# Twelve gate and up operands stored whole in the first half and split in place in the unit that reads them first

## The chip, the cores and the metric

One core of a Trainium2 chip runs the kernel. The metric is the device time of one execution in microseconds (us), the median of several. A core has five engines that work side by side, each through its own list of instructions in order: PE (matrix multiplications; the loading of its weights is shown apart, as PEld), DVE (vector), ACT (scalar functions, copies), POOL (a second vector engine) and SP, which here issues all DMA transfers. Engines wait for each other, and for transfers, at semaphores.

## The reference

A decoder block on a 2048 x 1024 input in float32: two token mixers in parallel, an output projection and a residual, and then the part that matters here, the gated feed-forward layer:

```python
h2 = rmsnorm(x, norm2_g[l])
ffn = (jax.nn.silu(h2 @ w_ffn_gate[l]) * (h2 @ w_ffn_up[l])) @ w_ffn_down[l]
x = x + ffn
return rmsnorm(x, norm_f_g)
```

`h2` is 2048 x 1024, `w_ffn_gate` and `w_ffn_up` are 1024 x 2816, `w_ffn_down` is 2816 x 1024.

## The kernel before

Every float32 operand of a matrix product is split in two numbers of a shorter format (fp32r): a high part, which ACT makes with a copy (line 153), and a low part, the difference, which DVE makes (line 154). One product is then three matmuls of 128 x 128 weights by 128 x 512 values (lines 391 to 393): high by high, high by low, low by high.

The large products are done in *units* (`unit`, L396): a product of two by two blocks from seven block products instead of eight. `PRODUCTS` names the seven pairs in their order: weights A11, S1, S2, A12, S3, S4, A22 with values B11, T1, T2, B21, T3, B22, T4. Each value operand is four tiles (k = 0 to 3) of 128 x 512, each held as a pair, 128 x 2 x 512, of high and low part, in the pool `opp` of 28 tiles: 7 x 4, so one set fills it. `unit_weights` loads a unit's raw weights by one transfer of 1 MB into one of two `raw` tiles, forms the sums on POOL (lines 374, 375, 376, 381) and splits seven weights into tiles `wq` (a pool of four). Copies of a block (line 413), sums of blocks (line 417) and, for the gate, a silu on ACT (line 452) end a unit.

The positions are done in two halves of 1024. `ffn_up(half)` runs 11 steps of two units each, gate and up; their product is split into `so` tiles (a pool of three, `fo`) by `store_split` and stored (`sa...`). `ffn_down(half)` follows. The second half's `h2` operands are made while `ffn_up(0)` runs: the generator `h2_ahead` is resumed once in four block products and calls `combine`, which for each k loads four blocks of x (`h`), scales them on DVE (line 520) and forms T1 to T4 on POOL (lines 269, 273, 276, 282). Each of the 28 results goes through `put`, which calls `store_split`: an ACT split and a DVE split into a `so` tile, and a store of 512 KB into the DRAM tile `sh<name>_<k>`. A round for one k has seven results: B11, T1, T2, T3, B21, T4, B22.

Between `ffn_down(0)` and `ffn_up(1)`, `load_h2` brings the 28 pairs back into `opp` tiles (28 loads of 512 KB). They are issued on SP among the stores of the first half's last results (`sx`) and the loads of raw weights, behind the raw load of the first gate unit.

The program text gives what is done; the order of each engine's list comes from a scheduler that sorts the instructions by an estimate of their times. It is fixed when the program is built. It lets the products of two neighbouring units overlap: at the place of the change PE's list has products of the up unit (marked ' below: A11', S1' and so on) between those of the gate unit.

In `in_proj` the first layer's operands T3, B22 and T4 (`WHOLE`) already travel whole: `h1_ahead` stores 256 KB, and `load_whole` (L566) loads them into the low part's place and splits them there.

Of the kernel before, what the change touches and what calls it, by code (L numbers as in the profile page):

```python
# [10 lines left out]
F32 = mybir.dt.float32  # L11
# [7 lines left out]
P = 128  # L19
D = 1024  # L20
SEQ = 2048
PB = 512
# [21 lines left out]
WHOLE = ("T3", "B22", "T4")  # L44
# [7 lines left out]
def tile_hymba_block(ctx, tc, x, xt, win, wa, wgu, wout, wffn, wdown, wdown_first, small, out):  # L52
# [3 lines left out]
    def pool_of(name, bufs, **kw):  # L56
        return ctx.enter_context(tc.tile_pool(name=name, bufs=bufs, **kw))
# [8 lines left out]
    dram = pool_of("dram", 1, space=DRAM)  # L66
# [34 lines left out]
    def scratch(name, n):  # L101
# [16 lines left out]
        for half in range(2)  # L118
    ]
    s_h2 = {n: [dram.tile([P, PB], F32, name=f"sf{n}_{k}") for k in range(4)] for n in LATER}  # L120
    s_h2p = {
        n: [dram.tile([P, 2, PB], F32, name=f"sh{n}_{k}") for k in range(4)] for _, n in PRODUCTS
    }

    def made_ahead(name, n):
        return dram.tile([P, PB] if n in WHOLE else [P, 2, PB], F32, name=name)

    s_h1 = {
        n: [made_ahead(f"si{n}_{k}", n) for k in range(4)] for _, n in PRODUCTS
    }  # L130
# [4 lines left out]
    def bank(name="mm"):  # L135
        return ps.tile([P, PB], F32, name=name, tag="mm")

    def tt(name):
        return tp.tile([P, PB], F32, name=name, tag="t")
# [4 lines left out]
    def load(dst, src):  # L144
        return nc.sync.dma_start(dst, src)

    def store(dst, src):
        return nc.sync.dma_start(dst, src)
# [3 lines left out]
    def split(src, hi, lo):  # L152
        last_hi[:] = [act.activation(hi, src, AF.Copy)]  # L153
        return dve.tensor_tensor(lo, src, hi.bitcast(F32), ALU.subtract)  # L154
# [20 lines left out]
    def both_rstd(ssq, rb):  # L175

        tot = [bank("tot") for _ in range(2)]
        for j in range(2):
            pe.matmul(tot[j][:], ones[:], ssq[j][:], start=True, stop=True)
        l, y0 = [[bt(n) for _ in range(2)] for n in ("l", "y0")]  # L180
        with tc.issue_after(last_silu[0].ins):
            last_exp[:] = [act.preload_act_table_set("natural_log_exp_and_others")]
        for j in range(2):
            with tc.issue_after(last_exp[0].ins):
                last_exp[:] = [
                    act.activation(l[j][:], tot[j][:], AF.Ln, bias=eps[:], scale=1.0 / D)
                ]
# [53 lines left out]
    def no_operands():  # L241
        return {b: [] for _, b in PRODUCTS}
# [125 lines left out]
    def unit_weights(src, raw=None):  # L368
        raw = raw_weights(src) if raw is None else raw
        n = src.shape[-1]  # L370
        a11, a12, a22, a21 = [raw[:, i, :] for i in range(4)]
        s1 = rawp.tile([P, PB], F32, name="s1", tag="s1", bufs=1)[:, 0:n]
        w = {"A11": weight_quarter(a11)}
        pool.tensor_tensor(s1, a21, a22, ALU.add)  # L374
        pool.tensor_tensor(a21, a11, a21, ALU.subtract)  # L375
        pool.tensor_tensor(a11, s1, a11, ALU.subtract)  # L376
        w["S1"] = weight_quarter(s1)
        w["S2"] = weight_quarter(a11)
        w["A12"] = weight_quarter(a12)
        w["S3"] = weight_quarter(a21)  # L380
        pool.tensor_tensor(a12, a12, a11, ALU.subtract)  # L381
        w["S4"] = weight_quarter(a12)
        w["A22"] = weight_quarter(a22)
        return w

    def product_step(o, w, op, k, first, s=slice(0, PB)):
        n = len(op)
        c = slice(k * P, (k + 1) * P)
        wh, wl = w[:, 0, c], w[:, 1, c]
        xh, xl = op[k][:, 0, s], op[k][:, 1, s]  # L390
        pe.matmul(o[:, s], wh, xh, start=first and k == 0, stop=False, skip_group_check=True)  # L391
        pe.matmul(o[:, s], wh, xl, start=False, stop=False, skip_group_check=True)  # L392
        return pe.matmul(o[:, s], wl, xh, start=False, stop=k == n - 1, skip_group_check=True)  # L393

    def unit(src, ops, into=None, raw=None, onto=None):


        w = unit_weights(src, raw)

        def mul(i, o=None):  # L400
            first = o is None
            o = bank() if first else o
            n, m = PRODUCTS[i]
            for k in range(len(ops[m])):
                product_step(o, w[n], ops[m], k, first)
            tick()
            return o

        def copied(name, o, at):
            if onto is not None:  # L410
                return plus(onto[at], o)
            t = tt(name) if into is None else into[at]
            act.activation(t[:], o[:], AF.Copy)  # L413
            return t

        def plus(t, o):
            dve.tensor_tensor(t[:], o[:], t[:], ALU.add)  # L417
            return t


        oa = mul(0)
        c11 = copied("c11", oa, (0, 0))
        ob = mul(1)
        c22 = copied("c22", ob, (1, 1))
        mul(2, oa)
        c12 = copied("c12", oa, (0, 1))
        plus(c11, mul(3))
        mul(4, oa)
        plus(c22, oa)
        mul(5, ob)  # L430
        plus(c12, ob)
        mul(6, oa)
        if into or onto:
            copied("c21", oa, (1, 0))
        return [(0, 0, c11, False), (1, 1, c22, False), (0, 1, c12, False), (1, 0, oa, True)]
# [6 lines left out]
        act.activation(s[:], c[:], AF.Copy)  # L442
        return s

    last_silu, last_exp = [], []

    def silu(c, in_psum):
        s = tt("sg") if in_psum else c
        with ExitStack() as stack:
            if last_exp:  # L450
                stack.enter_context(tc.issue_after(last_exp[0].ins))
            last_silu[:] = [act.activation(s[:], c[:], AF.Silu)]
        return s
# [440 lines left out]
    def h2_ahead(ssq):  # L894


        for _ in range(3):
            yield
        rb = [bank("rb_ps") for _ in range(2)]
        yield from both_rstd(ssq, rb)  # L900

        def put(n, k, h):
            store_split(s_h2p[n][k], h)

        yield from combine(lambda k, j: s_x1[2 + j][k][:], C_G2, rb, put)

    def load_h2():
        ops, loads = no_operands(), raw_loads[-1]
        for _, n in PRODUCTS:
            for k in range(4):  # L910
                o = opp.tile([P, 2, PB], F32R, name="op", tag="op")
                with tc.issue_after(loads.ins):
                    load(o[:].bitcast(F32), s_h2p[n][k][:])
                ops[n].append(o)
        return ops

    def ffn_up(half, ops, raw=None):
        for m in range(NF // 2):
            us = unit(wffn[2 * m], ops, raw=None if m else raw)
            sg = {(r, j): silu(c, p) for r, j, c, p in us}  # L920
            for r, j, c, _ in unit(wffn[2 * m + 1], ops):
                s = sg[r, j]
                dve.tensor_tensor(s[:], c[:], s[:], ALU.mult)
            b11, b12, b21, b22 = [sg[r, j] for r in range(2) for j in range(2)]
            t1, t2, t3, t4 = [bt(n) for n in ("t1", "t2", "t3", "t4")]
            for y, p, q in ((t1, b12, b11), (t2, b22, t1), (t3, b22, b12), (t4, b21, t2)):
                pool.tensor_tensor(y[:], p[:], q[:], ALU.subtract)  # L927
            values = [("B11", b11), ("B21", b21), ("B22", b22)]
            if half == 1 and m >= LAST_GROUP:
                values.append(("B12", b12))  # L930
            values += [("T1", t1), ("T2", t2), ("T3", t3), ("T4", t4)]
            background.insert(0, split_later(s_act[half][m], values))
# [235 lines left out]
    ops, first, differences = build_h()  # L1168
# [9 lines left out]
    ops = load_pairs(s_h1)  # L1178
# [124 lines left out]
```

## Time and profile before

| | us |
|---|---|
| median of 3 runs | 2085.23 |
| lowest and highest of them | 2084.04, 2087.19 |
| the profiled execution, its own time | 2085.32 |
| its span, first to last instruction | 2083.6 |
| PE busy in it | 2026.7 |
| DVE busy | 1429.0 |
| ACT busy | 965.2 |
| POOL busy | 882.6 |

Times in views of the trace count from the start of the span. In a row of a timeline stand the start, the duration, the engine, the line of the program, the operation, the tile written and those read, and in brackets the idle time of the engine just before and what ended it. `ffn_up(0)` with the making of the operands ahead lies at about 820 to 1130 us; the seam between the halves, where the operands are loaded, at about 1400 to 1456 us. Matmuls overlap: a row's duration is longer than the step from one start to the next.

### The profile page before, as it was taken

What the parts mean: (1) busy time and instruction counts of PE and PEld (TensorE: products, weight loads), DVE (VectorE), ACT (ScalarE), POOL (GpSimd) and SP (SyncE); (2) the same over time, 40 slices, a digit from 0 to 9 for tenths busy, and PEclk for the clock granted to TensorE, in tenths of its full rate; (3) what the DMA queues carried; (4) which work ended last, traced back from release to release, by engine and by line L of the source; (5) the groups of instructions that cost most, each with busy time, mean ns of one, the idle gap of its engine ahead of it and who ended that gap; (6) DMA issues with size and microseconds to landing.
All of it is one profiled execution on the core that took longest, in us unless ns stands there. A gap on an engine that the chain in (4) does not pass through costs nothing.

```text
span 2083.6 us, 26960 instructions
## 1 busy us (share of the span) xinstructions
PE 2026.7 (97%) x9175; PEld 1651.2 (79%) x9175; DVE 1429.0 (69%) x2057; ACT 965.2 (46%) x1918; POOL 882.6 (42%) x642
## 2 busy tenths in 40 slices
PE   5999999999999999999999999999999999999997
PEld 4778888887888887778888878887888888878886
DVE  7669786549754696787887566654776776666665
ACT  6455455656543245554555442223455444443234
POOL 3427322222102364555555434533655534534545
PEclk9999999999999999999999999999999999999999
DMA  7349495424586882654654587689454465398763
GB/s 277 126 152 313 145 342 160 152 96 137 182 304 206 331 295 96 234 218 175 237 222 163 211 344 275 237 328 361 167 185 159 177 227 202 136 354 318 288 263 121
DMA packets 190395, 464.45 MB, mean 223 GB/s; under 512 B 19952, under 2 KB 67248, under 8 KB 180656
## 3 DMA queue, kind: packets, MB, share of 16 engines
q1 hardware_dynamic: 190256, 462.72, 61.5%
q8 instruction: 72, 1.18, 0.2%
q14 instruction: 67, 0.55, 0.1%
HBM read 297.49 MB, written 165.15 MB: 222 GB/s over the span
## 4 chain that ended last, share of the span: by engine, by line
PE 79%; DVE 6%; DMA 3%; issue 2%; POOL 1%; ACT 1%; SPq 0%; DVEq 0%; POOLq 0%; ACTq 0%
PE mm L391 23%; PE mm L393 23%; PE mm L392 22%; PE mm L824 3%; PE mm L825 2%; PE mm L827 2%; DVE wq L154 2%; DVE so L154 1%; DMA raw<-in_wffn_dram 1%; DMA shT<-so 1%; PE o_ps L748 1%; PE o_ps L750 1%; DMA op<-sa_T 1%; PE sc L724 0%; POOL t L927 0%
## 5 line engine op out<-in xcount | busy, mean ns | idle before, releaser
L391 PE MATMUL mm<-op,wq 128*128 128x512 f32 x2511 | 982.1, 393 | 10.8 <-ACT c L413 5.0
L392 PE MATMUL mm<-op,wq 128*128 128x512 f32 x2511 | 977.3, 389 | 0.0
L393 PE MATMUL mm<-op,wq 128*128 128x512 f32 x2511 | 964.8, 390 | 10.4 <-DVE wq L154 10.2
L154 DVE TENSOR_TENSOR wq<-raw,wq 128x512 fp32r<-128x512 f32 (+2 forms) x626 | 503.0, 810 | 230.7 <-ACT wq L153 228.6
L153 ACT ACTIVATE wq<-raw 128x512 fp32r<-128x512 f32 (+2 forms) x626 | 363.8, 587 | 590.2 <-PE mm L393 456.2
L391 PEld LDWEIGHTS mm<-op,wq 128*128 128x128 f32 x2511 | 472.4, 188 | 122.7 <-ACT c L413 8.6
L393 PEld LDWEIGHTS mm<-op,wq 128*128 128x128 f32 x2511 | 472.5, 188 | 116.7 <-DVE wq L154 18.8
L392 PEld LDWEIGHTS mm<-op,wq 128*128 128x128 f32 x2511 | 472.7, 188 | 96.4 <-issue 1.2
L376 POOL TENSOR_TENSOR raw<-s,raw 128x512 f32<-128x512 f32 (+2 forms) x97 | 127.1, 1310 | 473.4 <-DVE wq L154 446.9
L417 DVE TENSOR_TENSOR y<-mm,y 128x512 f32<-128x512 f32 x185 | 127.2, 689 | 131.5 <-PE mm L393 131.2
L374 POOL TENSOR_TENSOR s<-raw 128x512 f32<-128x512 f32 (+2 forms) x97 | 128.0, 1320 | 205.3 <-DMA raw<-in_wffn_dram 101.4
L381 POOL TENSOR_TENSOR raw<-raw 128x512 f32<-128x512 f32 (+2 forms) x97 | 124.9, 1288 | 164.7 <-DVE wq L154 157.6
L417 DVE TENSOR_TENSOR c<-mm,c 128x512 f32<-128x512 f32 x198 | 135.3, 683 | 64.9 <-PE mm L393 63.6
L806 POOL TENSOR_TENSOR ssx<-ssx,q 128x512 f32<-128x512 f32 x52 | 76.1, 1478 | 161.6 <-ACT q L805 161.5
L375 POOL TENSOR_TENSOR raw<-raw 128x512 f32<-128x512 f32 (+2 forms) x97 | 135.8, 1400 | 5.3
L413 ACT ACTIVATE c<-mm 128x512 f32<-128x512 f32 x198 | 114.9, 587 | 17.3 <-PE mm L393 15.8
L154 DVE TENSOR_TENSOR so<-t,so 128x512 fp32r<-128x512 f32 x100 | 89.1, 896 | 25.2 <-ACT so L153 24.7
L153 ACT ACTIVATE wq<-s 128x512 fp32r<-128x512 f32 (+2 forms) x97 | 56.7, 585 | 95.9 <-PE mm L393 89.0
L824 PE MATMUL mm<-op,wq 128*128 128x512 f32 x256 | 100.9, 395 | 0.0
L825 PE MATMUL mm<-op,wq 128*128 128x512 f32 x256 | 99.8, 390 | 0.0
L154 DVE TENSOR_TENSOR wq<-s,wq 128x512 fp32r<-128x512 f32 (+2 forms) x97 | 81.1, 836 | 9.8 <-ACT wq L153 9.2
L153 ACT ACTIVATE so<-t 128x512 fp32r<-128x512 f32 x100 | 62.5, 627 | 41.6 <-DMA sa_B<-so 17.8
(188 smaller groups left out, 1847.9 us busy)
## 6 DMA issues: line engine op xcount, KB each, us to landing
raw<-in_wffn_dram SPq DMA_DIRECT2D x44, 1024.0 KB, 5.6
sa_T<-so SPq DMA_DIRECT2D x88, 512.0 KB, 5.3
op<-sa_T SPq DMA_DIRECT2D x88, 512.0 KB, 9.6
sa_B<-so SPq DMA_DIRECT2D x69, 512.0 KB, 3.4
op<-sa_B SPq DMA_DIRECT2D x69, 512.0 KB, 9.6
raw<-in_win_dram SPq DMA_DIRECT2D x23, 1024.0 KB, 5.5
raw<-in_wdown_dram SPq DMA_DIRECT2D x24, 768.0 KB, 6.2
sx<-y SPq DMA_DIRECT2D x48, 256.0 KB, 3.0
```

Of the source, the lines that this page charges most:

```text
L153: last_hi[:] = [act.activation(hi, src, AF.Copy)]
L154: return dve.tensor_tensor(lo, src, hi.bitcast(F32), ALU.subtract)
L374: pool.tensor_tensor(s1, a21, a22, ALU.add)
L375: pool.tensor_tensor(a21, a11, a21, ALU.subtract)
L376: pool.tensor_tensor(a11, s1, a11, ALU.subtract)
L381: pool.tensor_tensor(a12, a12, a11, ALU.subtract)
L391: pe.matmul(o[:, s], wh, xh, start=first and k == 0, stop=False, skip_group_check=True)
L392: pe.matmul(o[:, s], wh, xl, start=False, stop=False, skip_group_check=True)
L393: return pe.matmul(o[:, s], wl, xh, start=False, stop=k == n - 1, skip_group_check=True)
L417: dve.tensor_tensor(t[:], o[:], t[:], ALU.add)
L824: pe.matmul(o[e, j][:], wh, m[:, 0, :], start=k == 0, stop=False)
L825: pe.matmul(o[e, j][:], wh, m[:, 1, :], start=False, stop=False)
```

## The change

For T3, B22 and T4 (twelve of the 28 tiles) `put` no longer splits. The tile is stored as it is, 256 KB, into a DRAM tile of half the size. `load_h2` loads it into the low part's half of its `opp` tile. The split is made in the first unit that reads it, the gate unit of step 0 in the second half: a new dictionary `late` holds the four tiles of each name under the index of its product (4, 5, 6), and `mul(i)` calls `split_whole` on them just before the product. ACT writes the high part, and DVE overwrites the value with the low part.

```diff
+    s_h2p = {
+        n: [made_ahead(f"sh{n}_{k}", n) for k in range(4)] for _, n in PRODUCTS
+    }
...
             n, m = PRODUCTS[i]
+            split_whole(late.pop(i, ()))
             for k in range(len(ops[m])):
                 product_step(o, w[n], ops[m], k, first)
...
-    last_silu, last_exp = [], []
+    last_silu, last_exp, late = [], [], {}
...
         def put(n, k, h):
-            store_split(s_h2p[n][k], h)
+            if n in WHOLE:
+                store(s_h2p[n][k][:], h[:])
+            else:
+                store_split(s_h2p[n][k], h)
...
                 with tc.issue_after(loads.ins):
-                    load(o[:].bitcast(F32), s_h2p[n][k][:])
+                    load((o[:, 1, :] if n in WHOLE else o[:]).bitcast(F32), s_h2p[n][k][:])
                 ops[n].append(o)
         return ops
 
+    def split_whole(ops):
+        for o in ops:
+            split(o[:, 1, :].bitcast(F32), o[:, 0, :], o[:, 1, :])
+
     def ffn_up(half, ops, raw=None):
         for m in range(NF // 2):
+            if half and m == 0:
+                late.update({i + 2: ops[n] for i, n in enumerate(WHOLE)})
             us = unit(wffn[2 * m], ops, raw=None if m else raw)
```

The number of instructions on each engine is unchanged: twelve ACT and twelve DVE splits move from `ffn_up(0)` to the start of `ffn_up(1)`. The scheduler also sets some neighbours in another order. Three places are shown, first the list before, then the list now.

The first place is ACT's list in the first half, in the round of k = 0, from the split of an FFN step's T2 (`so<-t_7996`) to the silu at the end of its next gate unit. `so<-t_7897` is the operand T4 and `so<-h` the operand B22; `so<-t_7997` and `so<-t_7998` are the FFN step's own T3 and T4.

```order
L153 ACTIVATE so<-t_7996 128x512
L153 ACTIVATE wq<-s_8158 128x512
L153 ACTIVATE so<-t_7897 128x512
L452 ACTIVATE c_8082<-c_8082 128x512
L153 ACTIVATE wq<-raw 128x512
L452 ACTIVATE c_8063<-c_8063 128x512
L153 ACTIVATE so<-t_7997 128x512
L153 ACTIVATE wq<-raw 128x512
L153 ACTIVATE so<-t_7998 128x512
L153 ACTIVATE so<-h 128x512
L452 ACTIVATE sg<-mm 128x512
```

Now (the lines below the edit have moved by one, L452 to L453):

```order
L153 ACTIVATE so<-t_7996 128x512
L153 ACTIVATE wq<-s_8155 128x512
L153 ACTIVATE so<-t_7997 128x512
L453 ACTIVATE c_8079<-c_8079 128x512
L153 ACTIVATE wq<-raw 128x512
L453 ACTIVATE c_8063<-c_8063 128x512
L153 ACTIVATE so<-t_7998 128x512
L153 ACTIVATE wq<-raw 128x512
L453 ACTIVATE sg<-mm 128x512
```

The two operand splits are gone, and the FFN step's T3 and T4 have each moved up by one place.

The second place is ACT's list at the seam, from the gate unit's first silu (`c_12666`, now `c_12630`, the block c11) on. The `wq` rows behind it are the up unit's weights A11', S1', S2' and so on.

```order
L452 ACTIVATE c_12666<-c_12666 128x512
L153 ACTIVATE wq<-raw 128x512
L153 ACTIVATE wq<-s_12759 128x512
L153 ACTIVATE wq<-raw 128x512
L452 ACTIVATE c_12681<-c_12681 128x512
L153 ACTIVATE wq<-raw 128x512 x3
L452 ACTIVATE c_12695<-c_12695 128x512
L452 ACTIVATE sg<-mm 128x512
```

Now:

```order
L453 ACTIVATE c_12630<-c_12630 128x512
L153 ACTIVATE wq<-raw 128x512
L153 ACTIVATE op<-op 128x512 x5
L153 ACTIVATE wq<-s_12747 128x512
L153 ACTIVATE op<-op 128x512 x2
L153 ACTIVATE wq<-raw 128x512
L153 ACTIVATE op<-op 128x512 x2
L453 ACTIVATE c_12645<-c_12645 128x512
L153 ACTIVATE op<-op 128x512 x2
L153 ACTIVATE wq<-raw 128x512 x2
L453 ACTIVATE c_12667<-c_12667 128x512
L153 ACTIVATE op<-op 128x512
```

The twelve splits (`op<-op`: four of T3, four of B22, four of T4) stand between the up unit's weights, five of them ahead of S1'. DVE's list has its twelve in the same way: five ahead of S1', two ahead of the sum of c22, four after S2' and the last after S3'.

The third place is PE's list at the same time. `wq_12760` (now `wq_12748`) is A11' and `wq_12639` (now `wq_12603`) is S3; `op_12599` (now `op_12563`) is T3 of k = 0.

```order
L391 MATMUL mm_12785<-op_12567,wq_12760 128x512
L392 MATMUL mm_12785<-op_12567,wq_12760 128x512
L393 MATMUL mm_12785<-op_12567,wq_12760 128x512
L391 MATMUL mm_12785<-op_12569,wq_12760 128x512
L391 MATMUL mm_12649<-op_12599,wq_12639 128x512
L392 MATMUL mm_12649<-op_12599,wq_12639 128x512
L393 MATMUL mm_12649<-op_12599,wq_12639 128x512
```

Now:

```order
L391 MATMUL mm_12773<-op_12531,wq_12748 128x512
L392 MATMUL mm_12773<-op_12531,wq_12748 128x512
L391 MATMUL mm_12613<-op_12563,wq_12603 128x512
L393 MATMUL mm_12773<-op_12531,wq_12748 128x512
L391 MATMUL mm_12773<-op_12533,wq_12748 128x512
L392 MATMUL mm_12773<-op_12533,wq_12748 128x512
```

The first matmul that reads T3 has come forward from the fifth place to the third; it wants the high part alone. The other two of that tile follow at the fourteenth and fifteenth place, when A11' is through, and T3's other tiles after them.

More of the change, by code (lines that the diff above doesn't have):

```diff
@@ L120, in tile_hymba_block @@
     s_h2 = {n: [dram.tile([P, PB], F32, name=f"sf{n}_{k}") for k in range(4)] for n in LATER}
-    s_h2p = {
-        n: [dram.tile([P, 2, PB], F32, name=f"sh{n}_{k}") for k in range(4)] for _, n in PRODUCTS
-    }
     def made_ahead(name, n):
         return dram.tile([P, PB] if n in WHOLE else [P, 2, PB], F32, name=name)
+    s_h2p = {
+        n: [made_ahead(f"sh{n}_{k}", n) for k in range(4)] for _, n in PRODUCTS
+    }
     s_h1 = {
```

## The prediction

> **What bounds the kernel now.** I began with the head of the page and then had the matrix engine's own idle time listed along the whole span.
>
> ```profile
> span 2083.6 us, 26960 instructions
> PE 2026.7 (97%) x9175; PEld 1651.2 (79%) x9175; DVE 1429.0 (69%) x2057; ACT 965.2 (46%) x1918; POOL 882.6 (42%) x642
> PE mm L393 <- DVE wq L154: 3.0, 5, 0.9
> PE mm L391 <- ACT c L413: 1.7, 3, 0.9
> 855.55 0.50 PE L391 MATMUL mm<-op,wq 128*128 128x512 f32 x1 [0.53 <-ACT c L413]
> 887.12 0.50 PE L393 MATMUL mm<-op,wq 128*128 128x512 f32 x1 [0.75 <-DVE wq L154]
> 890.61 0.50 PE L391 MATMUL mm<-op,wq 128*128 128x512 f32 x1 [0.90 <-ACT c L413]
> 922.14 0.50 PE L393 MATMUL mm<-op,wq 128*128 128x512 f32 x1 [0.88 <-DVE wq L154]
> ```
>
> PE is busy for 97% of the span, so the change is worth what it takes from, or adds to, PE's idle time. The two waits rows (us in total, times, longest) cover 820 to 1130 us, in which the first half makes the second half's operands: PE idles there 3.0 + 1.7 = 4.7 us in eight stalls of 0.2 to 0.9 us, four of which follow. A first matmul after a stall shows 0.50 us, others 0.39: I add 0.11 us per stall.
>
> The operands are read where `ffn_up(1)` begins. Columns of the windows view: stretch, length, busy time of PE, its weight loads, DVE, ACT and POOL, granted clock, DMA share, GB/s.
>
> ```profile
> 1430.00:1435.00 5.00, 3.12 (x14) 2.25 (x12) 1.39 (x2) 2.24 (x4) 2.55 (x2) 1.00 1.02 412
> 1435.00:1440.00 5.00, 4.92 (x14) 3.61 (x15) 0.69 (x1) 0.03 (x1) 1.29 (x1) 0.67 1.02 411
> 1440.00:1445.00 5.00, 5.00 (x23) 4.15 (x22) 2.08 (x3) 1.90 (x3) 0.00 (x0) 0.99 1.03 415
> 1445.00:1450.00 5.00, 5.00 (x23) 4.14 (x23) 0.69 (x1) 0.63 (x1) 1.29 (x1) 1.00 1.02 414
> 1435.08 0.50 PE L391 MATMUL mm<-op,wq 128*128 128x512 f32 x1 [1.96 <-ACT wq L153]
> 1455.35 0.50 PE L391 MATMUL mm<-op,wq 128*128 128x512 f32 x1 [1.69 <-ACT c L413]
> 1433.88 0.63 ACT L452 ACTIVATE c<-c 128x512 f32<-128x512 f32 x1 [2.33 <-DVE c L417]
> 1434.42 0.61 ACT L153 ACTIVATE wq<-raw 128x512 fp32r<-128x512 f32 x1
> ```
>
> The DMA engines are full to 1450 (411 to 415 GB/s), yet neither stall of PE (1.96 and 1.69 us) ends on a load. The first ends on ACT: a silu waited for a sum on DVE (2.33 us), the split of the up unit's first weight stands behind it, and PE waits for that split. The second ends on a copy of ACT behind another silu.
>
> **What is removed in the first half.** For each of twelve operands the `so` pair goes: one ACT split, one DVE split, one of three `so` buffers held until its store lands, and 256 of 512 KB.
>
> ```profile
> L154 DVE TENSOR_TENSOR so<-t,so 128x512 fp32r<-128x512 f32 x100 | 89.1, 896 | 25.2 <-ACT so L153 24.7
> L153 ACT ACTIVATE so<-t 128x512 fp32r<-128x512 f32 x100 | 62.5, 627 | 41.6 <-DMA sa_B<-so 17.8
> 884.42 0.63 ACT L153 ACTIVATE so<-t 128x512 fp32r<-128x512 f32 x1 [2.38 <-DMA sa_T<-so]
> 884.96 0.61 ACT L153 ACTIVATE wq<-raw 128x512 fp32r<-128x512 f32 x1
> 887.15 0.63 ACT L153 ACTIVATE so<-t 128x512 fp32r<-128x512 f32 x1 [1.57 <-DMA sa_T<-so]
> 888.43 0.63 ACT L153 ACTIVATE so<-h 128x512 fp32r<-128x512 f32 x1 [0.65 <-DMA shT<-so]
> 888.97 0.58 ACT L452 ACTIVATE sg<-mm 128x512 f32<-128x512 f32 x1
> 889.97 0.59 ACT L413 ACTIVATE c<-mm 128x512 f32<-128x512 f32 x1
> 886.39 0.68 DVE L154 TENSOR_TENSOR wq<-raw,wq 128x512 fp32r<-128x512 f32 x1
> ```
>
> That is 12 x 0.90 = 10.8 us of DVE and 12 x 0.63 = 7.5 us of ACT; but only what ends one of the eight stalls counts. I went through them with the new order. The rows show the worst pair. At 884.42 ACT waited 2.38 us for a store to leave a `so` buffer; at 887.15 another 1.57; at 888.43 (B22 of k = 0, `so<-h`) 0.65 more. Behind these stands the silu, behind that the copy at 889.97, which ends the 0.90 us stall at 890.61. In the new order T4's and B22's pairs are gone from here, T3 of the FFN stage takes the buffer that T4 held, and its T4 the one that came free at 884.42. ACT is then through with splits at 885.05 instead of 889.06, and the copy waits for PE alone. That stall goes: 0.90 + 0.11 = **1.0 us**.
>
> The stall at 887.12 stays: its weight split (DVE 886.39) follows ACT's 884.96, which still follows a split that gets its buffer at 884.42. That at 855.55 comes before T3 would have been split. That at 922.14, and its like in the later rounds, waits for a weight behind two T1 splits on DVE (an FFN value's and an operand's); both stay, and the new order has the same two and one sum ahead of that weight. The early whole stores (B22's and T3's, 256 KB each) now share DMA with the stores on which ACT waits. At 411 GB/s they take 0.64 us each; at worst each of four rounds loses that, 2.6 us, at best the freed DVE clears all eight stalls, 4.7 + 8 x 0.11 = 5.6 us. I take -1.0.
>
> **What is added at the seam.** Twelve ACT and twelve DVE splits, in place, stand among the weight splits of the up unit.
>
> ```profile
> 1422.63 0.32 SPq L145 DMA_DIRECT2D op<-shT  x1
> op<-shT SPq DMA_DIRECT2D x1, 512.0 KB, 10.7
> 1435.06 0.69 DVE L154 TENSOR_TENSOR wq<-raw,wq 128x512 fp32r<-128x512 f32 x1 [1.21 <-ACT wq L153]
> 1440.75 0.63 ACT L153 ACTIVATE wq<-s 128x512 fp32r<-128x512 f32 x1 [5.72 <-PE mm L393]
> 1441.41 0.69 DVE L154 TENSOR_TENSOR wq<-s,wq 128x512 fp32r<-128x512 f32 x1 [5.66 <-ACT wq L153]
> 1443.20 0.69 DVE L417 TENSOR_TENSOR c<-mm,c 128x512 f32<-128x512 f32 x1 [1.10 <-PE mm L393]
> 1442.24 0.32 SPq L145 DMA_DIRECT2D op<-shT  x1
> op<-shT SPq DMA_DIRECT2D x1, 512.0 KB, 10.4
> 1452.75 0.44 PE L391 MATMUL mm<-op,wq 128*128 128x512 f32 x1
> 1453.03 0.39 PE L392 MATMUL mm<-op,wq 128*128 128x512 f32 x1
> ```
>
> By the DVE row a split takes 0.69 us, so 8.3 us in all; ACT's twelve take 7.6. From 1435 to 1450 DVE is busy 3.5 us and ACT 2.6 (the windows rows): there is room for three times as much. Order matters more, as ACT and DVE take their lists in order. T3 of k = 0, issued at 1422.63, lands 10.7 us later, at 1433.3, before ACT is through with the weight (1434.95). Its high part is there at 1435.6; PE's third matmul, which now wants it, ran at about 1435.8. Four T3 and one B22 split then stand before the weight of S1 on ACT, 5 x 0.53 = 2.7 us to 1437.7; that weight waits for PE until 1440.75 anyway (5.72 us idle). On DVE the same five end at about 1435.7 + 5 x 0.69 = 1439.2, before 1441.41. Two B22 splits come before the c22 sum of 1443.20: 1440.7 + 0.69 for the weight + 1.38 = 1442.8. B22's last and three of T4 follow; DVE reaches them from 1444; PE, 32 matmuls of 0.24 us after its fourteenth at 1440 (rows under the first rival), from about 1447. T4's last part is the tightest. Today its load, issued behind a 1 MB weight load at 1442.24, lands 10.4 us later, at 1452.6, and PE reads it at 1452.75. But the loads ahead of it are twelve of half size: 12 x 0.64 = 7.7 us less for the full DMA engines, so it lands at about 1445 and its split waits only in ACT's list, behind a weight that wants B22's last matmul and a silu, until about 1450. Hence **0 us** here. The covers are DVE's and ACT's idle time and those 7.7 us; were they gone, see the third rival.
>
> DVE is not always that quick:
>
> ```profile
> 912.59 1.61 POOL L276 TENSOR_TENSOR h<-h 128x512 f32<-128x512 f32 x1 [1.35 <-DVE h L520]
> 912.97 1.78 DVE L154 TENSOR_TENSOR so<-c,so 128x512 fp32r<-128x512 f32 x1
> ```
>
> A split beside a POOL operation took 1.78 us, 1.1 more. Two POOL operations lie in the stretch (x1 and x1 in the windows rows) and two come forward with the next weights: 4.4 us at most, spread over slacks of 1.5 us and more.
>
> [...]
>
> The sum: 2083.6 - 1.0 + 0 = 2082.6 us of span. The profiled execution took 2085.32 us, 1.7 more than its span and 0.1 more than the median of 2085.23: 2082.6 + 1.7 - 0.1 = **2084.2 us**.
>
> **The rivals.**
>
> *The clock spares the seam.* The 1435 row grants 0.67.
>
> ```profile
> 1436.96 0.63 PE L393 MATMUL mm<-op,wq 128*128 128x512 f32 x1
> 1440.26 0.40 PE L393 MATMUL mm<-op,wq 128*128 128x512 f32 x1
> 1440.50 0.39 PE L391 MATMUL mm<-op,wq 128*128 128x512 f32 x1
> ```
>
> Eight matmuls from 1436.96 to 1440.26 took 3.30 us; at 0.24 (the next step) they take 1.9, so the slow spell cost 1.4 us. It follows the 1.96 us stall; the 1.69 us stall has none, so a little decides it. Without it: 2084.2 - 1.4 = 2082.8.
>
> [...]
>
> *The whole first half is freed.* All eight stalls go, 5.6 us: 2079.6. For it speaks that ACT's list waits for `so` stores (2.38, 1.57 and 0.65 us in the rows); against it, that the other stalls I placed stand at work that stays.
>
> *T4 comes late.* If half-size loads pace as full ones do (their cost is in their number), T4's last part lands at 1452.6 still, and now needs 0.63 on ACT and up to 1.78 on DVE: 1455.0, where PE wanted it at 1453.03. A stall of 2.0 us, as long as the one that brought a slow spell, for another 1.4; the chain to the copy at 1455.35 shifts along. If the 1.0 us is not earned either: 2085.2 + 3.4 = 2088.6. It decides once the load lands after about 1450.5. Against it: rows of 256 KB (`sx`) stand in the same queue, and the full engines move bytes.
>
> *Nothing moves.* Other waits for `so` take the place of the one removed: 2085.2.
>
> **How the numbers follow.** Forecast 0.36; spared clock 0.14; all stalls gone 0.14; T4 late 0.22; nothing 0.08; a stall not listed 0.06. A difference under 0.2% (4.2 us) is what a measurement of this kernel can hardly tell from none, so faster means under 2081.1, slower over 2089.4. Faster: most of the third case, and a little of the second and the sixth, 0.21. Slower: half of the late T4, whose price grows with each contended split ahead, and most of what is not listed, 0.17. Within: 0.62. Range 2080.3 to 2088.9; the forecast's own is 2082.5 to 2085.5.
>
> **What would show it.** Right: no stall at 890, and those at 887 and 922 as before; the full-DMA stretch ends near 1443; the twelve `op<-op` splits stand in it without PE waiting for `op`; 1.96 and 1.69 us stalls remain. Wrong: PE rows that end on `op` of DVE or ACT after 1435, a longer slow spell there, or stalls near 846 to 856 grown by the early stores.

## The result, and the profile after

The changed kernel takes 2081.09 us (median of 17 runs, 2077.84 to 2084.03) against 2084.29 us for the kernel before in the same session (17 runs, 2082.67 to 2088.97). The ratio over all runs is 0.9982, 95% interval 0.9974 to 0.9989: 3.8 us less, 2.3 to 5.4 (the two medians differ by 3.2). The forecast was 2084.2 us with a range of 2080.3 to 2088.9. The sign and the range held; the size was too small, and the forecast's own band, 2082.5 to 2085.5, does not reach down to the measured time.

The head of the page after, and PE's waits between 820 and 1130 us (us in total, times, longest):

```profile
span 2079.4 us, 26961 instructions
PE 2027.7 (98%) x9175; PEld 1653.1 (79%) x9175; DVE 1430.9 (69%) x2057; ACT 965.0 (46%) x1918; POOL 880.0 (42%) x642
PE mm L391 <- ACT c L414: 2.7, 4, 1.5
PE mm L393 <- DVE wq L154: 0.3, 1, 0.3
```

The span is 2079.4 us for 2083.6. In the first half the waits on weights fell from 3.0 to 0.3 us, but those on ACT's copies rose from 1.7 to 2.7. The stalls, in PE's timeline after:

```profile
853.73 0.50 PE L391 MATMUL mm<-op,wq 128*128 128x512 f32 x1 [0.55 <-ACT c L414]
926.25 0.50 PE L391 MATMUL mm<-op,wq 128*128 128x512 f32 x1 [1.50 <-ACT c L414]
1003.19 0.50 PE L391 MATMUL mm<-op,wq 128*128 128x512 f32 x1 [0.34 <-ACT c L414]
1430.61 0.50 PE L391 MATMUL mm<-op,wq 128*128 128x512 f32 x1 [1.97 <-ACT wq L153]
1431.93 0.80 PE L393 MATMUL mm<-op,wq 128*128 128x512 f32 x1 [0.30 <-DVE wq L154]
1451.13 0.50 PE L391 MATMUL mm<-op,wq 128*128 128x512 f32 x1 [1.69 <-ACT c L414]
```

The 853.73 stall is that of 855.55 before. Those of 887, 890 and 922 us are gone, not the 890 one alone. One of 1.50 us has come at 926 us. The two at the seam stand as they were (1.97, 1.69), with 0.30 us beside the first in this trace.

The seam in the windows view after (length, then PE, weight loads, DVE, ACT, POOL, granted clock, DMA share, GB/s), and the added splits as the tile view groups them (durations in ns, shortest, median, longest):

```profile
1430.00:1435.00 5.00, 4.09 (x10) 2.96 (x11) 4.41 (x5) 3.27 (x7) 2.88 (x2) 0.69 1.02 374
1435.00:1440.00 5.00, 5.00 (x23) 4.07 (x22) 4.14 (x8) 3.02 (x6) 0.00 (x0) 0.97 0.89 352
1440.00:1445.00 5.00, 5.00 (x24) 4.14 (x23) 3.94 (x8) 3.17 (x7) 1.21 (x1) 1.00 0.05 19
L153 ACT ACTIVATE op<-op x12: 613/616/630, 1430.5 to 1445.5; 128x512 fp32r<-128x512 f32 x12
L154 DVE TENSOR_TENSOR op<-op x12: 675/684/1766, 1431.8 to 1446.2; 128x512 fp32r<-128x512 f32 x12
```

The DMA engines empty at about 1439, which is 9 us behind the seam's first stall; before it was 15 (1450 against 1435.08). All twelve splits lie between 1430.5 and 1447.3 us and no PE row ends on `op`. The slow spell, a stretch at half the granted clock, is there (0.50 from 1431.9 to 1435.3 us, 0.69 over the first row).

One thing in the description above has to be put right: `late` holds T3, B22 and T4 under the indices 2, 3 and 4 (`i + 2` in the diff), so the program text splits them two products ahead of the one that reads them, not just before it. The lists quoted there show what the scheduler made of it, and the sum was made from the lists.

### The profile page after: what moved, and what is told of

Its sections match the earlier page's. It is cut to its first block, busy times and chain, and to the rows that moved or that the text cites. A ratio compares the mean times of both kernels' runs of the same rounds, so it can differ in the third digit from the quotient of the medians.

```text
span 2079.4 us, 26961 instructions
## 1 busy us (share of the span) xinstructions
PE 2027.7 (98%) x9175; PEld 1653.1 (79%) x9175; DVE 1430.9 (69%) x2057; ACT 965.0 (46%) x1918; POOL 880.0 (42%) x642
## 4 chain that ended last, share of the span: by engine, by line
PE 86%; DVE 7%; DMA 4%; issue 2%; ACT 1%; POOL 1%; SPq 0%; DVEq 0%; ACTq 0%; POOLq 0%
PE mm L391 25%; PE mm L393 24%; PE mm L392 24%; PE mm L825 3%; PE mm L826 2%; PE mm L828 2%; DVE wq L154 2%; DVE op L154 1%; DMA op<-sa_T 1%; DVE so L154 1%; PE a_ps L589 1%; DMA raw<-in_wdown_dram 1%; PE o_ps L749 1%; DVE h L521 1%; PE o_ps L751 1%
## 5 line engine op out<-in xcount | busy, mean ns | idle before, releaser
L154 DVE TENSOR_TENSOR wq<-raw,wq 128x512 fp32r<-128x512 f32 (+2 forms) x626 | 503.5, 810 | 235.5 <-ACT wq L153 233.9
L154 DVE TENSOR_TENSOR so<-t,so 128x512 fp32r<-128x512 f32 x96 | 91.2, 954 | 24.0 <-ACT so L153 23.7
L154 DVE TENSOR_TENSOR wq<-s,wq 128x512 fp32r<-128x512 f32 (+2 forms) x97 | 78.9, 813 | 4.9 <-ACT wq L153 4.4
```

## The experiments

One profile is one execution, so I cut each into stretches between PE stalls that nearly all executions have: the weight stall near 786 us, the sum stall near 1227, the first seam stall on a weight near 1433, the sum stall near 1867. Beside two stretches stands the number of half-clock spells that lie in them. All in us, from PE's timeline and the granted clock; the last column is the ratio to the kernel before with its interval, where it was timed.

| kernel | to 786 | 786 to 1227 | 1227 to 1433 | 1433 to 1867 | ratio |
|---|---|---|---|---|---|
| before | 786.93 | 441.84 (0) | 206.31 | 434.21 (1) | |
| before, second | 785.57 | 442.35 (1) | 205.75 | 435.47 (2) | |
| before, third | 787.46 | 441.20 (0) | 205.61 | 435.40 (2) | |
| changed | 785.22 | 439.50 (0) | 205.89 | 433.74 (1) | 0.9982 (0.9974 to 0.9989) |
| changed, second | 787.31 | 439.94 (0) | 205.59 | 433.90 (1) | |
| changed, third | 789.24 | 441.25 (1) | 205.60 | 433.40 (1) | |
| first half only | 785.59 | 438.56 (0) | 205.70 | 436.76 (2) | 0.9991 (0.9982 to 0.9999) |
| seam only | 784.33 | 440.41 (0) | 206.18 | 432.94 (1) | 0.9986 (0.9977 to 0.9996) |
| T3 alone | 785.79 | 440.30 (0) | 205.89 | 431.83 (0) | |
| B22 alone | 787.67 | 440.85 (1) | 205.85 | 433.79 (1) | |
| T4 alone | 785.87 | 441.31 (1) | 206.15 | 437.39 (2) | |
| four names | 786.85 | 440.69 (1) | 206.42 | 431.93 (0) | 0.9975 (0.9966 to 0.9984) |
| B22 and T4 | 786.66 | 440.83 (1) | 206.01 | 436.44 (2) | 1.0006 (0.9995 to 1.0017) |
| four `so` buffers | 785.36 | 439.76 (0) | 206.02 | 434.47 (1) | |

And PE's stalls in the first half, by their place on before's clock (us):

| kernel | 846 to 857 | 887 | 890 | 922 | 926 | 999 to 1083 | sum |
|---|---|---|---|---|---|---|---|
| before, three traces | 1.06, 0.87, 1.15 | 0.75, 0.46, 0.73 | 0.90, 0.48, 0.45 | 0.88, 0.88, 0.88 | 0 | 1.11, 1.12, 1.13 | 4.70, 3.81, 4.34 |
| changed, three traces | 0.89, 0.89, 0.84 | 0 | 0 | 0 | 1.50, 1.95, 1.97 | 0.66, 0.59, 0.33 | 3.05, 3.43, 3.14 |
| first half only | 0.89 | 0 | 0 | 0 | 1.07 | 0.35 | 2.31 |
| seam only | 0.83 | 0.72 | 0 | 0.89 | 0 | 1.11 | 3.55 |
| T3 alone | 0.89 | 0 | 0 | 0.88 | 1.03 | 1.14 | 3.94 |
| B22 alone | 0.90 | 0.70 | 0 | 0 | 0 | 0.38 | 1.98 |
| T4 alone | 0.85 | 0.47 | 0 | 0.88 | 0 | 1.12 | 3.32 |
| four names | 0.32 | 0 | 0 | 0 | 1.41 | 1.49 | 3.22 |
| B22 and T4 | 0.90 | 0.60 | 0 | 0 | 0 | 0 | 1.50 |
| four `so` buffers | 0 | 0 | 0 | 0.77 | 0 | 1.39 | 2.16 |

### The same kernels again

No edit: the kernel before and the changed one, each twice more.

> The kernel before, unchanged, for a second trace. The two traces in hand differ by 4.2 us of span, of which 1.7 us are there at the matmul at 786.9 us (before) and 785.2 us (now), ahead of any edit. Theory A: those 1.7 us are the spread of one execution to another; in this trace the stalls up to 787 us then add up to another sum than the 29 us of the first trace, by up to 2 us either way, while the eight stalls between 846 and 1077 us (4.7 us) and the two at the seam (1.96 and 1.69 us) come out within 0.3 us of the first trace, since they hang on the order of the lists. Rival B: the early part repeats to 0.2 us, so the change earns 1.7 us there in some way that the lists do not show. Rival C: the eight stalls wander by more than 1.5 us too, and then a single pair of traces says little about the first half.

> The changed kernel, unchanged, for a second trace. Theory A: the first half again shows some 3.05 us of stalls between 840 and 1045 us with the largest, about 1.5 us, near 926 us on a copy of ACT (L414), and the seam 1.97, 0.30 and 1.69 us; the early part differs. Rival C: the 1.5 us stall, or those of 887, 890 and 922 us that went, turn up here in other sizes.

> The kernel before once more, for a third trace. Theory K (a stall at the seam starts half-clock spells that cost 1.71 us each, 0 to 2 of them, by chance, and without a spell the last T4 load holds the seam at 20 us): the seam, from the matmul behind its first stall to that behind its copy stall, takes 20.2 to 22.1 us, and there is no such thing as 18.4 us. Rival L (the seam of before can be as short as that of the kernel with T3 alone): under 19.5 us.

> The changed kernel once more, for a third trace. Theory K: the same stretch takes 18.4 us without a spell or 19.9 to 20.5 with one; the first half again has the stall near 926 us (1.5 and 1.95 us so far) and 370.9 to 371.5 us between its two landmarks. Rival L: 20 us and more whatever the clock does.

Theory A holds for the start: up to the stall near 786 us the kernel before took 785.6 to 787.5 us, the changed one 785.2 to 789.2. The 1.7 us that the first pair of traces showed there was spread. The order-bound stalls repeat to 0.01 us (0.88 at 922, 1.97 and 1.69 at the seam), those that hang on a store's landing do not (0.45 to 0.90 at 890), so the 0.3 us that I allowed for the sum of the eight was too little. The 0.30 us beside the first seam stall, which I expected to see again, is in neither of the other two traces of the changed kernel.

Theory K holds in what it says of a spell and in the length of the seam (20.3 us in before's third trace, 20.0 in the changed kernel's), not in its number for the first half. Between the landmarks lost clock comes in one size: the granted clock is 0.50 for 3.41 us (before's third trace: 1434.43 to 1437.84), so 1.71 us are lost. After the first seam stall before's second trace has two such spells back to back, where the first trace had one:

```profile
1430.00:1435.00 5.00, 2.44 (x10) 1.39 (x8) 2.42 (x3) 1.29 (x3) 2.54 (x2) 0.93 1.03 412
1435.00:1440.00 5.00, 4.95 (x12) 3.90 (x13) 0.00 (x0) 0.00 (x0) 1.27 (x1) 0.50 1.03 416
1440.00:1445.00 5.00, 5.00 (x21) 4.07 (x20) 1.98 (x3) 1.85 (x3) 0.00 (x0) 0.89 1.03 413
```

The third trace of before has one there and one after the copy stall at 1454.60. The three traces of the changed kernel have one each, so none of them shows the 18.4 us without a spell. And one followed the new stall too, which took the third trace's first half out of the stretch expected (372.7 us between its two landmarks):

```profile
930.74 0.50 PE L391 MATMUL mm<-op,wq 128*128 128x512 f32 x1 [1.97 <-ACT c L414]
931.00:935.00 4.00, 4.00 (x12) 3.15 (x12) 3.25 (x6) 1.33 (x3) 0.22 (x1) 0.61 0.63 213
```

### One half of the change at a time

The first edit stores the twelve tiles whole and loads each of them twice; it leaves out their split. The second leaves the first half as it was before the change, loads the stored high parts of the twelve alone and splits those; it leaves out their low parts.

```diff
-                    load((o[:, 1, :] if n in WHOLE else o[:]).bitcast(F32), s_h2p[n][k][:])
+                    if n in WHOLE:
+                        for e in range(2):
+                            load(o[:, e, :].bitcast(F32), s_h2p[n][k][:])
+                    else:
+                        load(o[:].bitcast(F32), s_h2p[n][k][:])
...
-                late.update({i + 2: ops[n] for i, n in enumerate(WHOLE)})
```

```diff
-        n: [made_ahead(f"sh{n}_{k}", n) for k in range(4)] for _, n in PRODUCTS
+        n: [dram.tile([P, 2, PB], F32, name=f"sh{n}_{k}") for k in range(4)] for _, n in PRODUCTS
...
-            if n in WHOLE:
-                store(s_h2p[n][k][:], h[:])
-            else:
-                store_split(s_h2p[n][k], h)
+            store_split(s_h2p[n][k], h)
...
-                    load((o[:, 1, :] if n in WHOLE else o[:]).bitcast(F32), s_h2p[n][k][:])
+                    if n in WHOLE:
+                        load(o[:, 1, :].bitcast(F32), s_h2p[n][k][:, 0, :])
+                    else:
+                        load(o[:].bitcast(F32), s_h2p[n][k][:])
```

> The first half of the change alone: the twelve tiles are stored whole, and each is loaded twice, into the high and the low part's place, so that the seam moves the bytes that it moved before; their split is left out, so twelve operands enter as twice their value. Theory A (the gain comes from the first half): PE's stalls between 840 and 1130 us fall from 4.7 us to some 3, the 890 us stall is gone, and the ratio is 0.9988 or lower, like the whole change's 0.9982. Rival D (the gain is the lighter loads at the seam): the ratio is within 0.0004 of 1. Rival E (the splits at the seam cost something that the first half pays for): the ratio is lower than 0.9978.

> The seam's part alone: the first half splits and stores all 28 pairs as before, and the second half loads only the stored high parts of the twelve (256 KB each) and splits those in place; the low parts are left out. Theory A: the first half shows its 4.7 us of stalls, the seam 1.97 + 0.30 + 1.69 us, and the ratio lies within 0.0004 of 1. Rival D (lighter loads at the seam earn the gain): ratio 0.9985 or lower. Rival F (the splits at the seam cost, which the first half pays for): over 1.0004.

Both halves earn: 1.9 us (0.2 to 3.8) and 2.9 us (0.8 to 4.8), from the ratios and the 2086.7 us of the kernel before in that session. The first half's ratio, 0.9991, misses theory A's 0.9988 by a little, with the interval (0.9982 to 0.9999) on both sides of it. For the seam theory A falls by its ratio (it said within 0.0004 of 1, and the interval ends at 0.9996); rival D is as good as met at 0.9986, but the first half alone is no tie either.

What the seam earns is for the most part clock. The granted clock of each timed execution is on record. It averages 0.9949 over the twelve of seam only and 0.9938 over the 23 of the kernel before beside them; the difference is 2.4 us of the span (interval 1.2 to 3.6), most of the 2.9 us. First half only has 0.9934, so its gain is not in the clock. For the changed kernel it is 0.9945 over 17 executions against 0.9939 over 52 of the kernel before in the three later sessions (0.9938 to 0.9943 each): about 1.1 us (0.2 to 2.0). Why a lighter seam loses less clock is not shown.

The traces of seam only and of the changed kernel also tell something of the 890 us stall. ACT's silu in that round, in the changed kernel, and the split of B22 ahead of that silu, in seam only:

```profile
883.75 0.60 ACT L453 ACTIVATE sg<-mm 128x512 f32<-128x512 f32 x1 [1.41 <-PE mm L393]
884.76 0.63 ACT L153 ACTIVATE so<-h 128x512 fp32r<-128x512 f32 x1 [1.20 <-DMA shT<-so]
```

In the changed kernel ACT waits for PE there, as the sum said, and does not hold PE up. But seam only still makes all 28 pairs, its B22 split waited 1.20 us for a buffer, and the stall is missing from it all the same. With all pairs in place the stall was thus 0.90, 0.48, 0.45 and 0 us in four traces.

The first half alone also shows what the lighter loads do. Its clock stayed whole after the first seam stall, and this happened:

```profile
1429.85 0.50 PE L391 MATMUL mm<-op,wq 128*128 128x512 f32 x1 [1.97 <-ACT wq L153]
1447.76 0.49 PE L391 MATMUL mm<-op,wq 128*128 128x512 f32 x1 [1.69 <-DMA op<-shT]
1450.83 0.80 PE L391 MATMUL mm<-op,wq 128*128 128x512 f32 x1 [1.69 <-ACT c L414]
1440.00:1445.00 5.00, 5.00 (x22) 3.86 (x21) 1.68 (x4) 1.33 (x3) 1.30 (x1) 1.00 1.04 408
```

PE ran into the last load of T4 (1.69 us, on `op<-shT`) while the DMA engines were full to 1445, and two spells lie back to back from about 1450 us on: 436.76 us for the stretch, the longest but one. In this trace, with the bytes that the seam moved before the change, the spared clock was worth nothing, since PE got to T4 ahead of its load.

### One name at a time, and other sets of names

In all of these the first layer's `WHOLE` stays; a second tuple says which names of `h2` go whole, and `late` keeps its distance of two products. For T3 alone:

```diff
+LATE = ("T3",)
...
-            if n in WHOLE:
+            if n in LATE:
                 store(s_h2p[n][k][:], h[:])
...
-                late.update({i + 2: ops[n] for i, n in enumerate(WHOLE)})
+                late.update({i - 2: ops[n] for i, (_, n) in enumerate(PRODUCTS) if n in LATE})
```

> Only T3's four tiles are stored whole and split at the seam. Theory A (ACT's waits for so buffers make the stalls; the new 1.5 us stall near 926 us comes from whole stores that are issued early and take the DMA engines from the so stores): T3's whole store of k = 1 is one of the two early ones, so a stall of 0.5 us or more on a copy of ACT appears near 925 us, while that of 887 us (0.5 to 0.75 us) stays or shrinks by less than half. Rival G (the splits' time on ACT and DVE is what counts, not the buffers): a third of the pairs gone gives a third of the fall in every stall, and no new stall.

> Only B22's four tiles are stored whole and split at the seam. Theory A: the pair that waited at 888.43 us in the first trace is gone, so the stall at 890 us is under 0.3 us; B22's whole store is the other early one, and the new stall near 925 us is there with 0.3 us or more. Rival G: a third of the fall in every stall and no new one.

> Only T4's four tiles are stored whole and split at the seam. Theory A: T4's pair, which held a so buffer for FFN values behind it, is gone: the 890 us stall is under 0.3 us; T4's whole stores come late in their rounds, so no new stall of ACT near 925 us; the 922 us stall on a weight (0.88 us) stays. At the seam T4 is lighter by 4 x 256 KB only, and its last split ends before PE wants it: stalls 1.97 and 1.69 us and no third over 0.7 us. Rival G as above.

> The change widened to B21: sixteen tiles stored whole and split at the seam, one product further ahead. Theory A (both halves pay: fewer so pairs in the first half, fewer bytes at the seam): between 855 and 1228 us it takes 370 to 371.4 us (before 373.2 and 372.3 in two traces, the change 371.0 and 371.4), the full-DMA stretch of the seam ends about 2.6 us earlier than the change's, and the ratio is 0.9975 to 0.9988. Rival H (the seam's ACT and DVE have no room for four more pairs): a PE stall over 0.5 us that ends on op of ACT or DVE after 1428 us, and a ratio over 0.9988.

> The change without T3: B22 and T4 stored whole and split at the seam. Theory A (B22's pair frees the stalls at 887 to 1077 us, T4's that at 890, and T3's early whole store makes the new stall near 926 us): the first half shows stalls of 1.2 us or less between 840 and 1130 us, none near 926, and takes 370.0 to 370.9 us from the copy stall near 854 to that near 1227 us (the change 371.0 and 371.4); at the seam 2 MB less is loaded, 5.1 us of full engines, so T4's last split is done in time and the seam's stalls are 1.97 and 1.69 us with 0.7 us beside them at most; ratio 0.9970 to 0.9982. Rival J (T3's bytes are needed too, else T4 comes late as it does in the run with T4 alone): a stall over 0.7 us on op near 1450 us and a ratio over 0.9985.

Rival G (every pair is worth a third) is out: the names do different things. The 887 us stall goes with T3, against theory A: it is 0 in all six traces in which T3 is whole in the first half, and 0.46 to 0.75 us in the seven others with three buffers. The `so<-t` split of 884.42 us, which waits for a store to leave its buffer, begins 28.9 us behind the stall near 854 us in before's first trace, 27.5 in the changed kernel's and 27.2 with T3 alone. The 922 us stall goes with B22 and with nothing else in the table but sets that hold it. The 926 us stall is there in every trace in which T3 is whole in the first half (six: changed three times, first half only, T3 alone, four names) and in none of the others, B22's early store notwithstanding, which theory A had taken for a second cause. How the stall comes is in ACT's timeline of the changed kernel:

```profile
921.58 0.64 ACT L153 ACTIVATE so<-t 128x512 fp32r<-128x512 f32 x1 [1.53 <-DMA sa_T<-so]
922.83 0.63 ACT L153 ACTIVATE so<-t 128x512 fp32r<-128x512 f32 x1 [0.62 <-DMA shT<-so]
924.07 0.63 ACT L153 ACTIVATE so<-t 128x512 fp32r<-128x512 f32 x1
924.61 0.58 ACT L453 ACTIVATE sg<-mm 128x512 f32<-128x512 f32 x1
925.60 1.08 ACT L414 ACTIVATE c<-mm 128x512 f32<-128x512 f32 x2
```

ACT waits 1.53 and 0.62 us for stores to leave `so` buffers, the silu and the copy stand behind, and PE waits for the copy at 926.25. With B22 alone the like splits wait for nothing. The stores are slower, not later in the list; the tile view of `so` has their time to landing between 905 and 927 us here, then in the like stretch with B22 alone (910 to 932) and before (909 to 931):

```profile
DMA to landing us min/median/max: 2.6/5.0/7.2
DMA to landing us min/median/max: 2.6/3.5/5.2
DMA to landing us min/median/max: 2.6/2.9/4.5
```

Medians of 5.0, 3.5 and 2.9 us. In the like stretches of three more traces they are 4.8 (changed, second) and 4.2 (T3 alone) with T3 whole, 3.7 (B22 and T4) without. T3's whole store is issued just ahead of a 1 MB weight load and these stores; whether its bytes or the order of the issues slows them was not tried.

What B22 does at 922 is plain from DVE's list. Before, with the POOL operations that run beside it:

```profile
917.79 2.38 DVE L154 TENSOR_TENSOR so<-t,so 128x512 fp32r<-128x512 f32 x2
917.94 1.68 POOL L376 TENSOR_TENSOR raw<-s,raw 128x512 f32<-128x512 f32 x1 [3.75 <-DVE wq L154]
920.09 0.68 DVE L417 TENSOR_TENSOR c<-mm,c 128x512 f32<-128x512 f32 x1
920.25 1.28 POOL L273 TENSOR_TENSOR t<-h,t 128x512 f32<-128x512 f32 x1 [0.63 <-DVE so L154]
920.69 1.39 DVE L154 TENSOR_TENSOR wq<-s,wq 128x512 fp32r<-128x512 f32 x1
```

After:

```profile
913.57 0.68 DVE L154 TENSOR_TENSOR so<-t,so 128x512 fp32r<-128x512 f32 x1
913.72 1.69 POOL L376 TENSOR_TENSOR raw<-s,raw 128x512 f32<-128x512 f32 x1 [3.74 <-DVE wq L154]
914.17 0.68 DVE L418 TENSOR_TENSOR c<-mm,c 128x512 f32<-128x512 f32 x1
914.83 1.12 DVE L154 TENSOR_TENSOR so<-t,so 128x512 fp32r<-128x512 f32 x1
915.88 0.68 DVE L154 TENSOR_TENSOR wq<-s,wq 128x512 fp32r<-128x512 f32 x1
```

These are the same two splits, sum and weight split. Before, the two splits stand side by side and meet POOL, then the weight's split meets the next one: 4.3 us from 917.79 to 922.08. Now the sum stands between the splits and runs beside POOL at its usual 0.68 us: 3.0 us. The 1.3 us are more than the 0.88 us stall. The trace with T3 alone has before's order (2.39 us for the two) and the stall, that with B22 alone has the new order and no stall. All of before's first trace says the same of splits and sums of this size: 471 DVE splits (L154) stood clear of POOL and took 0.66 to 0.70 us; of the 336 that ran beside a POOL operation 224 took over 0.75, up to 1.82 us. The sums of L417, which read a matmul's result (`mm`), took 0.67 to 0.69 us beside POOL (184 of them) and 0.66 to 0.69 clear of it (199). Why these are spared is not shown.

At the seam, T4 alone (the first row) and B22 with T4 (the others) are the two slow ones, each with a stall on `op` over the 0.7 us that I had expected at most:

```profile
1451.83 0.65 PE L396 MATMUL mm<-op,wq 128*128 128x512 f32 x1 [1.66 <-DVE op L158]
1443.65 5.79 DVE L158 TENSOR_TENSOR op<-op 128x512 fp32r<-128x512 f32 x4
1443.88 1.62 POOL L385 TENSOR_TENSOR raw<-raw 128x512 f32<-128x512 f32 x1 [8.28 <-DVE wq L158]
1445.63 1.55 POOL L378 TENSOR_TENSOR s<-raw 128x512 f32<-128x512 f32 x1
1447.27 1.63 POOL L379 TENSOR_TENSOR raw<-raw 128x512 f32<-128x512 f32 x1
1449.37 0.68 DVE L422 TENSOR_TENSOR c<-mm,c 128x512 f32<-128x512 f32 x1
1450.61 0.61 ACT L157 ACTIVATE op<-op 128x512 fp32r<-128x512 f32 x1
1451.28 0.50 PE L395 MATMUL mm<-op,wq 128*128 128x512 f32 x1 [1.05 <-ACT op L157]
```

With B22 and T4 the loads were in by 1445 (DMA share 0.90 in the 5 us before, 0.01 in the 5 behind). But four splits on DVE met three POOL operations and took 5.79 us, the sum behind them came late, the silu behind that, T4's last split on ACT behind the silu, and PE waited 1.05 us. With T4 alone its splits stand behind a weight split on ACT that waits for PE (ACT: 0.00 us busy from 1445 to 1448); DVE's split for that stall comes at 1451.10, when the DMA engines are empty (0.12 from 1447 to 1448, 0.00 from 1450 on). So rival J's stall is there, and with B22 and T4 its cause is not the bytes, which were in: it is T4's place in ACT's list. The first half of that kernel is the cleanest of all (1.50 us of stalls, over the 1.2 forecast, since the 887 us stall stayed), yet its ratio is 1.0006. The stalls at the seam are not the whole of that: its granted clock averages 0.9930 against 0.9943 for the kernel before in that session, 2.7 us (1.2 to 4.2). Four names have the lowest ratio, 0.9975; its interval overlaps that of the change (to 0.9984 against from 0.9974), so whether it is the better one is not settled. Its clock is the highest, 0.9953 against 0.9939 beside it. There rival H was seen in small: in the place of the 1.97 us stall stand two on `op` of DVE (0.36 and 0.73 us) and one on a weight (0.49 us), and no spell followed them.

### A fourth buffer

```diff
-        for n, bufs in (("fx", 11), ("fo", 3))
+        for n, bufs in (("fx", 9), ("fo", 4))
```

> The kernel before with four so buffers in place of three; the room is taken from the pool beside it, which has nine tiles in place of eleven. Nothing else is edited. Theory A (ACT waits for a store to leave a so buffer, and the stalls hang on that wait): ACT's idle time ended by stores (16.6 + 6.2 + 5.1 us ahead of so<-t between 820 and 1130 us) falls by half or more, and the eight stalls fall from 4.7 us to under 2.5. Rival G (the time of the splits counts, not the buffers): the stalls at 887, 922 and 999 us stay at 0.5 us or more each, 4 us in all.

```profile
L153 ACT ACTIVATE so<-t 128x512 fp32r<-128x512 f32 x44 | 27.5, 627 | 18.7 <-DMA sa_B<-so 6.0 <-DMA shT<-so 5.7 <-POOL t L273 3.1
PE mm L393 <- DVE wq L154: 2.2, 3, 0.8
```

Each theory has its part. The stalls sum to 2.16 us, under theory A's 2.5. With a fourth buffer those from 846 to 890 us are gone: they hang on stores. Those at 922 and later stay (0.77 and 1.39 us), so they do not hang on the buffers alone; DVE has the two splits side by side there too, 0.68 and 1.56 us long beside POOL. Of ACT's idle time ahead of `so<-t`, what stores ended fell from 27.9 to 12.3 us, by more than half as expected. But ahead of `so<-h` it rose from 2.4 to 10.0, so that ACT waited 22.3 us for stores in all, where it was 31.1. The pool beside it lost two tiles, which this run does not separate.

## Why the prediction was right, and where it was not

- **The first half, forecast -1.0.** From 786 to 1227 us the three traces of before average 441.8 us, those of the change 440.2, with one spell among each three: -1.6. PE's stalls between 840 and 1130 us fell by 1.1 us in the mean, 1.4 with 0.11 us for each of the three that are gone. The step that ends in the 890 us stall was right in its mechanism: ACT waits for PE there in the changed kernel. Its size was not: 0.90 us is the largest of before's three, their mean is 0.61, and seam only lacks the stall with all its pairs. "That at 887.12 stays" was wrong: the fourth-buffer run shows that it hangs on the same `so` stores, and the table that it goes with T3's pair, without which the split at 884.42 gets its buffer 1.4 us sooner. "That at 922.14 ... both stay" was wrong in its inference: I had the right four operations on DVE (two splits, a sum and the weight's split) and took their order for indifferent. The order decides which of them meets POOL. That the total came near is in part luck, since these two stalls went while a new one came.
- **The early stores, bounded at 2.6 us.** They came, and not spread over four rounds but as one stall of 1.5 to 2.0 us in one round, which is T3's making, and 0.3 in the next, which T3 alone does not show. The stalls of 846 to 857 us did not grow (1.03 to 0.87 in the means). So the term was a difference of two larger ones: 887, 890, 922 and half of the last group gone (in the means 0.65, 0.61, 0.88 and 0.59), 926 come (1.81).
- **The seam, forecast 0.** The working held: no PE row ends on `op`, the splits fit, the DMA engines emptied when said (1443 on before's clock; 1439 here, where the seam began 4.5 us earlier). With the spells taken out at 1.71 us each, 1433 to 1867 takes 432.2 us before and 432.0 after. As executed it is 435.0 and 433.7, -1.3, since before lost five spells in its three traces and the change three. Three traces of each cannot tell that from chance, but the granted clocks of the timed executions speak against chance: seam only gains 2.4 us of clock and the whole change about 1.1. So the term put at 0 was missing the clock; why spells are fewer is not shown.
- **The clock spared, priced at -1.4.** A whole spell costs 1.71 us, not the 1.4 that I read from eight matmuls. The rival also needs the lighter loads, which I did not see: with the bytes of before, a spared clock ran PE into T4's load (first half only, one trace: a 1.69 us stall, then two spells). With lighter loads it can be earned: T3 alone and four names, without a spell, have 431.8 and 431.9 us. The changed kernel had its spell in all three traces.
- **T4 late, priced at +3.4.** It did not happen in the changed kernel. Where it did (T4 alone, B22 with T4: 437.4 and 436.4 us against before's 435.0; 434.0 and 433.0 against 432.2 with two spells taken out of each) the split was late in ACT's list, and not the load, as the price had assumed.
- **The sum.** -1.6 and -1.3, with -0.2 between them, 0.6 and 0.2 the other way in the start and the end, where nothing was edited, make -2.3 us in the mean of three spans (2083.8 to 2081.4). The timed runs say -2.3 to -5.4. Both terms were mis-sized: -1.0 measured -1.6, and 0 measured about -1.3 as executed, nearly all of it clock. That the range held owes something to chance: it was wide enough for a gain that the forecast did not work out.

## What to carry to other kernels

What a vector split cost here depended on what stood beside it on POOL: 0.66 to 0.70 us clear of it, up to 1.82 beside it, where a sum that reads a matmul's result took 0.67 to 0.69. So look at the order of the two lists and put such a sum where POOL is busy, before counting how many splits can be taken away. A transfer that is just hidden by a slow spell is a limit, as one trace here shows (1.69 us on T4's load when the clock stayed at 1.00): make it lighter before hoping for the clock. Write-behind buffers couple ACT to the queue of stores, so a store that is made smaller but issued earlier can still cost a stall: with T3's store halved ACT waited 1.53 and 0.62 us for `so` buffers, and PE 1.50 us behind it at 926 us.

## What the hardware showed that I had not expected

Half-clock spells came whole: in the six traces whose granted clock was read from end to end (two of before, two of the changed kernel, four `so` buffers, B22 and T4) it is 0.50 for 3.4 us, 1.70 to 1.72 us of lost time, or for twice that, two spells back to back; only behind the last matmul, at the end of the span, does it stay at 0.50 for longer (over 8 us in the first traces of before and of the changed kernel). The same stall of 1.96 to 1.97 us at the seam was followed by a spell at once in nine of thirteen traces and not in four; what decides it is not shown. Spells are not all that spreads the executions of one kernel. The three traces of the changed kernel span 2079.4, 2081.1 and 2083.8 us, and 4.0 of these 4.4 us are there at the stall near 786 us (785.2, 787.3, 789.2).
